# The last products of a two-layer trunk cut 384 and 128 tokens, with the final norm's weights multiplied on ScalarE

## The chip, the cores and the metric

The kernel runs on one core of a Trainium2 chip. The metric is the device time of one execution in microseconds (us), as the median of several runs. The profile shows one execution; its engines are PE (TensorE, matmuls), PEld (TensorE's weight loads, which overlap matmuls), DVE (VectorE), ACT (ScalarE), POOL (GpSimd) and SP (SyncE, here the queue that issues nearly all transfers).

## The reference

An input of 512 tokens x 1024 features passes through two layers: a token mixer (attention in the first, a gated recurrence in the second) and a squared-ReLU MLP after each. All of it is in float32. Only the end matters here, the second half of the last MLP and the final norm:

```python
def rmsnorm(x, g):
    y = xf * lax.rsqrt(jnp.mean(xf * xf, axis=-1, keepdims=True) + RMS_EPS)
    return (y * g.astype(jnp.float32)).astype(x.dtype)

    z = jax.nn.relu(jnp.einsum('bsd,df->bsf', h, w1))
    return jnp.einsum('bsf,fd->bsd', z * z, w2)      # D_FF = 4096
...
        h = h + sq_relu_mlp(rmsnorm(h, norm_mlp[layer]), mlp_w1[layer], mlp_w2[layer])
    return rmsnorm(h, norm_final)
```

## The kernel before

Features lie on the 128 partitions and tokens along the free dimension: the residual is eight tiles `hT[0..7]` of 128 features x 512 tokens. Every float32 operand of a product is split into a high part and a low rest, so one product of two blocks is three matmuls (`mm3`, lines 180 to 182), each with a weight load of 128 x 128 of its own.

An MLP runs over eight groups `g` of 512 hidden units. For each group `up(g)` makes the hidden units and `down(g - 1, m)` adds the group before it to the residual, with one projection for each feature tile `m` (line 624). In the last MLP the eighth group's down projection is written out apart (lines 665 to 689), because the final norm and the output follow it. The code is written in program order, and a scheduler orders the instructions of each engine in it from what they depend on.

There the 512 tokens are cut in two halves of 256 (`norms`, line 667). For each half and each tile `m` the projection makes 4 x 3 matmuls into one of four accumulator buffers (tag `mm`), VectorE adds the result to `hT` (line 685), and `Norm.square` squares it on ScalarE and adds it to a running sum on VectorE (lines 208 to 216). The last tile's square of the second half is made on VectorE and goes into the sums by matmuls of its own (`apart`, line 212; `last`, line 213).

`finish` then makes the norm of a half. `sums` adds over the features with matmuls against ones (line 232), ScalarE takes the root (line 236) and VectorE the reciprocal (line 237). `rstd` spreads the result over the partitions as a row with a matmul (line 243); for the first half ScalarE copies the row out of PSUM (line 247), for the second VectorE reads it there. For each tile VectorE multiplies residual, weight and row in one instruction (line 677), and after two tiles SP issues a store of 256 KB (line 678). The first half's `finish` comes after the second tile of the second half, and the second half's after everything. The running sums of both halves share one buffer (tag `nacc`).

Of the kernel before, what the change touches and what calls it, by code (L numbers as in the profile page):

```python
# [10 lines left out]
F32 = mybir.dt.float32  # L11
F32R = mybir.dt.float32r
AF = mybir.ActivationFunctionType
ALU = mybir.AluOpType

P = 128
T = 512
D = 1024
KT = D // P
NH = 16  # L20
HD = 64
U = 256
# [9 lines left out]
C_MIX0, C_MLP0, C_MIX1, C_MLP1, C_FIN = 0, 8, 16, 24, 32  # L32
# [8 lines left out]
def trunk(ctx: ExitStack, tc: tile.TileContext, xT, cols, win, wqkv, wo, rwin, rga, rgx, rwo, w1, w2, out):  # L41
    nc = tc.nc
    V, S, G, PE = nc.vector, nc.scalar, nc.gpsimd, nc.tensor
# [8 lines left out]
    def mmp(name):  # L52
        return ps.tile([P, T], F32, name=name, tag="mm")
# [5 lines left out]
    cst = per.tile([P, P], F32, name="cst")  # L59
    hT = [per.tile([P, T], F32, name=f"hT{k}") for k in range(KT)]  # L60
# [123 lines left out]
    def project(accs, cols_, WH, WL, xs, mid=None):  # L184

        for k, (XH, XL) in enumerate(xs):
            if mid and k == len(xs) // 2:
                mid()
            for acc, c in zip(accs, cols_):
                mm3(acc, WH(k, c), WL(k, c), XH, XL, k == 0, k == len(xs) - 1)  # L190
# [62 lines left out]
    with ExitStack() as actx:  # L253
# [169 lines left out]
        for k0, nk in FIRST:  # L423
            WH, WL = want(1)
            for k in range(k0, k0 + nk):
# [4 lines left out]
                for i in range(4):  # L430
                    c = slice(i * P, (i + 1) * P)
# [94 lines left out]
    def mlp(ly, norm, nxt, halves):  # L526
        with ExitStack() as mctx:
            pool = lambda name, bufs: mctx.enter_context(tc.tile_pool(name=f"{name}{ly}", bufs=bufs))
            sr, wx, tp, cp, zp = pool("sr", 1), pool("wx", 3), pool("t", 1), pool("c", 1), pool("z", 2)
# [123 lines left out]
            for g in range(1, 8):  # L653
                m = 0
# [9 lines left out]

            ws = [want(1) for u in range(4)]
            tc.keep_in_program_order(S.activation(spare, epsb, AF.Sqrt))
            norms = [Norm(f"nf{h}", C_FIN, h * U, U) for h in range(2)]

            def finish(nf):
                nf.sums()  # L670
                rf = nf.rstd()
                for m in range(0, KT, 2):
                    o = sr.tile([P, 1024], F32, name=f"{nf.name}o{m}", tag=("b11", "b21", "b22", "b12")[m // 2])
                    o = o[:, :T].rearrange("p (i c) -> p i c", i=2)
                    for i in range(2):
                        g = cst[:, C_FIN + m + i : C_FIN + m + i + 1]
                        V.scalar_tensor_tensor(o[:, i], hT[m + i][:, nf.c], g, rf, ALU.mult, ALU.mult)
                    nc.sync.dma_start(out[m * P : (m + 2) * P, nf.c].rearrange("(k p) c -> p k c", p=P), o)

            for h, nf in enumerate(norms):  # L680
                for m in range(KT):
                    acc = mmp(f"d{ly}7{m}{h}")[:, :U]
                    WH, WL = ws[m // 2]
                    project([acc], [PAIR[m % 2]], WH, WL, [(z[7, k][0][:, nf.c], z[7, k][1][:, nf.c]) for k in range(4)])
                    V.tensor_add(hT[m][:, nf.c], acc, hT[m][:, nf.c])
                    nf.square(m, h == 1 and m == KT - 1)
                    if h and m == 1:
                        finish(norms[0])
            finish(norms[1])

    n1 = Norm("n1", C_MIX1)
    mlp(0, nm1, n1.feed, False)


    nm2 = Norm("nm2", C_MLP1, late=True)
    with ExitStack() as rctx:
# [83 lines left out]
        for u in range(4):  # L780
            WH, WL = want(2)
            for i in range(2):
                c = 2 * u + i
                if i == 1 and u < 3:
                    gate_weights(u + 1)
                acc = mmp(f"xb{c}")
# [13 lines left out]
        for u in range(4):  # L800
            WH, WL = want(2)
            for i in range(2):
                c = 2 * u + i
# [15 lines left out]
        for u in range(4):  # L819
            WH, WL = want(2)  # L820
            accs = [mmp(f"ro{2 * u + i}") for i in range(2)]
            for i in range(2):
                m = 2 * u + i
# [5 lines left out]
                nm2.feed(m)  # L829

    mlp(1, nm2, None, True)


# [35 lines left out]
```

## Time and profile before

| | |
|---|---|
| median of 3 runs | 1092.68 us (1092.35 to 1092.8) |
| the profiled execution | 1092.29 us, of which the span from the first to the last instruction is 1090.5 us |
| busy share of the span | PE 99%, PEld 87%, DVE 79%, ACT 49%, POOL 1% |
| granted TensorE clock, mean of the span | 0.997 of full speed |
| transfers | 109 MB in 113784 packets |

A matmul's row shows its start and a modelled length that overlaps the next; the distance from one start to the next tells what it costs in a stream. The rows below give times from the start of the span. In a timeline row stand the start, the length, the engine, the line, the operation, the tiles written and read, and the shapes, partitions x elements; for PE the shape after the arrow is what is moved. Rows that say x4 merge four neighbours.

### The profile page before, as it was taken

What the parts mean: (1) busy time and instruction counts of PE and PEld (TensorE: products, weight loads), DVE (VectorE), ACT (ScalarE), POOL (GpSimd) and SP (SyncE); (2) the same over time, 40 slices, a digit from 0 to 9 for tenths busy, and PEclk for the clock granted to TensorE, in tenths of its full rate; (3) what the DMA queues carried; (4) which work ended last, traced back from release to release, by engine and by line L of the source; (5) the groups of instructions that cost most, each with busy time, mean ns of one, the idle gap of its engine ahead of it and who ended that gap; (6) DMA issues with size and microseconds to landing.
All of it is one profiled execution on the core that took longest, in us unless ns stands there. A gap on an engine that the chain in (4) does not pass through costs nothing.

```text
span 1090.5 us, 15782 instructions
## 1 busy us (share of the span) xinstructions
PE 1074.5 (99%) x6280; PEld 951.5 (87%) x6280; DVE 857.6 (79%) x1284; ACT 534.1 (49%) x778; POOL 10.5 (1%) x28
## 2 busy tenths in 40 slices
PE   9999999999999999999999999899999999999996
PEld 7889989878999999899988888788998999999896
DVE  7997888879777786786776889969777777786765
ACT  7766666566443443342344688446343443443321
POOL 1000000000000000000000000000000000000000
PEclk9999999999999999999999999999999999999998
DMA  8532432341432323322242222531532432322102
GB/s 270 138 100 76 116 104 71 95 156 48 146 116 78 109 91 109 98 84 91 78 135 59 78 71 65 168 122 58 156 97 78 124 102 84 109 91 90 61 1 78
DMA packets 113784, 109.08 MB, mean 100 GB/s; under 512 B 4016, under 2 KB 110640, under 8 KB 113712
## 3 DMA queue, kind: packets, MB, share of 16 engines
q1 hardware_dynamic: 113568, 108.02, 32.5%
q8 instruction: 49, 0.80, 0.3%
q14 instruction: 23, 0.19, 0.1%
q10 hardware_dynamic: 144, 0.07, 0.0%
HBM read 101.78 MB, written 2.10 MB: 95 GB/s over the span
## 4 chain that ended last, share of the span: by engine, by line
PE 87%; DVE 8%; ACT 2%; DMA 1%; issue 1%; DVEq 0%; SPq 0%; ACTq 0%
PE d L180 11%; PE d L181 11%; PE d L182 10%; PE p L182 9%; PE p L181 9%; PE p L180 9%; DVE wl L119 1%; PE u L180 1%; PE xb L180 1%; PE xb L182 1%; PE u L182 1%; PE u L181 1%; PE xb L181 1%; PE x L380 1%; PE wo L181 1%
## 5 line engine op out<-in xcount | busy, mean ns | idle before, releaser
L118 ACT CAST wh<-wr 128x1024 fp32r<-128x1024 f32 (+1 forms) x129 | 134.4, 1044 | 217.2 <-PE d L181 95.1
L181 PE MATMUL d<-zL,wh 128*128 128x512 f32 (+1 forms) x544 | 205.7, 379 | 0.0
L180 PE MATMUL d<-zH,wh 128*128 128x512 f32 (+1 forms) x544 | 205.5, 379 | 0.0
L182 PE MATMUL d<-zH,wl 128*128 128x512 f32 (+1 forms) x544 | 204.5, 377 | 0.0
L118 ACT CAST wh<-b 128x1024 fp32r<-128x1024 f32 x98 | 101.8, 1051 | 164.6 <-PE p L181 91.1
L119 DVE TENSOR_TENSOR wl<-wr,wh 128x1024 fp32r<-128x1024 f32 (+1 forms) x129 | 156.6, 1214 | 26.5 <-ACT wh L118 22.5
L119 DVE TENSOR_TENSOR wl<-b,wh 128x1024 fp32r<-128x1024 f32 x98 | 118.7, 1222 | 35.3 <-ACT wh L118 35.2
L182 PE MATMUL p<-tH,wl 128*128 128x256 f32 x448 | 126.8, 283 | 0.0
L181 PE MATMUL p<-tL,wh 128*128 128x256 f32 x448 | 126.8, 283 | 0.0
L180 PE MATMUL p<-tH,wh 128*128 128x256 f32 x448 | 126.6, 282 | 0.0
L182 PEld LDWEIGHTS d<-zH,wl 128*128 128x128 f32 x544 | 102.4, 188 | 19.4
L180 PEld LDWEIGHTS d<-zH,wh 128*128 128x128 f32 x544 | 102.5, 189 | 17.0 <-ACT zH L570 0.4
L181 PEld LDWEIGHTS d<-zL,wh 128*128 128x128 f32 x544 | 102.7, 189 | 15.7
L624 DVE TENSOR_TENSOR hT<-d,hT 128x512 f32<-128x512 f32 x120 | 82.6, 688 | 42.5 <-PE d L182 42.0
L182 PE MATMUL p<-hnH,wl 128*128 128x256 f32 x336 | 95.1, 283 | 0.0
L181 PE MATMUL p<-hnL,wh 128*128 128x256 f32 x336 | 95.1, 283 | 0.0
L180 PE MATMUL p<-hnH,wh 128*128 128x256 f32 x336 | 94.9, 282 | 0.0
L181 PEld LDWEIGHTS p<-tL,wh 128*128 128x128 f32 x448 | 85.8, 192 | 1.6
L180 PEld LDWEIGHTS p<-tH,wh 128*128 128x128 f32 x448 | 85.8, 192 | 1.6
L182 PEld LDWEIGHTS p<-tH,wl 128*128 128x128 f32 x448 | 85.8, 192 | 0.0
L181 PEld LDWEIGHTS p<-hnL,wh 128*128 128x128 f32 x336 | 64.3, 191 | 1.6
L180 PEld LDWEIGHTS p<-hnH,wh 128*128 128x128 f32 x336 | 64.3, 191 | 1.6
(334 smaller groups left out, 2146.5 us busy)
## 6 DMA issues: line engine op xcount, KB each, us to landing
wr<-in_w SPq DMA_DIRECT2D x72, 512.0 KB, 3.5
b<-in_w SPq DMA_DIRECT2D x56, 512.0 KB, 4.5
wr<-in_wqkv SPq DMA_DIRECT2D x20, 512.0 KB, 4.0
wr<-in_rwin SPq DMA_DIRECT2D x16, 512.0 KB, 3.5
wr<-in_wo SPq DMA_DIRECT2D x8, 512.0 KB, 3.5
wr<-in_rwo SPq DMA_DIRECT2D x8, 512.0 KB, 3.5
hT<-in_xT SPq DMA_DIRECT2D x8, 256.0 KB, 4.8
bias<-in_win SPq DMA_DIRECT2D x4, 512.0 KB, 4.4
```

What stands on the lines that cost most here:

```text
L118: S.copy(H[:, :n], raw[:, :n])
L119: V.tensor_sub(L[:, :n], raw[:, :n], f(H[:, :n]))
L180: PE.matmul(acc, WH, XH, start=start, stop=False)
L181: PE.matmul(acc, WH, XL, start=False, stop=False)
L182: PE.matmul(acc, WL, XH, start=False, stop=stop)
L380: PE.transpose(b[:, c : c + P], pt[:, seg[t] + kt * P : seg[t] + (kt + 1) * P], ident)
L624: V.tensor_add(hT[m], acc, hT[m])
```

## The change

The last down projection's cut becomes 384 and 128 tokens. The multiplication by the final norm's weights moves ahead of the norm: as soon as a tile of the residual is final, ScalarE writes tile x weight into the output buffer (`scale`). `finish` then multiplies the buffer by the row only, in place, over several feature tiles at once: two tiles x 384 tokens in the first part, four tiles x 128 tokens in the second. The first part's four buffers are the same as before, now 768 columns each; the second part uses the two buffers `cA` and `cB` of the hidden units. The first part's four stores are issued on SP's queue. Of the second part's two stores of 256 KB the first is issued on SP's queue and the second on ScalarE's.

```diff
-            norms = [Norm(f"nf{h}", C_FIN, h * U, U) for h in range(2)]
-
-            def finish(nf):
+            cuts = ((0, T - P), (T - P, P))
+            norms = [Norm(f"nf{h}", C_FIN, c0, n) for h, (c0, n) in enumerate(cuts)]
+
+            def finish(nf, step):
                 nf.sums()
                 rf = nf.rstd()
-                for m in range(0, KT, 2):
-                    o = sr.tile([P, 1024], F32, name=f"{nf.name}o{m}", tag=("b11", "b21", "b22", "b12")[m // 2])
-                    o = o[:, :T].rearrange("p (i c) -> p i c", i=2)
-                    for i in range(2):
-                        g = cst[:, C_FIN + m + i : C_FIN + m + i + 1]
-                        V.scalar_tensor_tensor(o[:, i], hT[m + i][:, nf.c], g, rf, ALU.mult, ALU.mult)
-                    nc.sync.dma_start(out[m * P : (m + 2) * P, nf.c].rearrange("(k p) c -> p k c", p=P), o)
+                for n, m in enumerate(range(0, KT, step)):
+                    o = scaled[nf][m // step]
+                    V.tensor_mul(o, o, rf[:, None, :].to_broadcast([P, step, nf.n]))
+                    eng = nc.scalar if nf.last is not None and n else nc.sync
+                    eng.dma_start(out[m * P : (m + step) * P, nf.c].rearrange("(k p) c -> p k c", p=P), o)
+
+            def scale(nf, m):
+
+                o = scaled[nf]
+                step = KT // len(o)
+                S.activation(o[m // step][:, m % step], hT[m][:, nf.c], AF.Copy, scale=cst[:, C_FIN + m : C_FIN + m + 1])
+
+            scaled = {norms[0]: [], norms[1]: []}
+            for m, tag in enumerate(("b11", "b21", "b22", "b12")):
+                o = sr.tile([P, 1024], F32, name=f"nf0o{m}", tag=tag)[:, : 2 * (T - P)]
+                scaled[norms[0]].append(o.rearrange("p (i c) -> p i c", i=2))
+            for m, tag in enumerate(("cA", "cB")):
+                o = cp.tile([P, 2, T], F32, name=f"nf1o{m}", tag=tag)[:, 0]
+                scaled[norms[1]].append(o.rearrange("p (i c) -> p i c", i=4))
 
             for h, nf in enumerate(norms):
                 for m in range(KT):
-                    acc = mmp(f"d{ly}7{m}{h}")[:, :U]
+                    acc = mmp(f"d{ly}7{m}{h}")[:, : nf.n]
                     WH, WL = ws[m // 2]
                     project([acc], [PAIR[m % 2]], WH, WL, [(z[7, k][0][:, nf.c], z[7, k][1][:, nf.c]) for k in range(4)])
                     V.tensor_add(hT[m][:, nf.c], acc, hT[m][:, nf.c])
                     nf.square(m, h == 1 and m == KT - 1)
+                    scale(nf, m)
                     if h and m == 1:
-                        finish(norms[0])
-            finish(norms[1])
+                        finish(norms[0], 2)
+            finish(norms[1], 4)
```

## Rows read from the trace of the kernel before

**Rows 1.** The page: busy time of each engine, share of the span, instructions.
```profile
PE 1074.5 (99%) x6280; PEld 951.5 (87%) x6280; DVE 857.6 (79%) x1284; ACT 534.1 (49%) x778; POOL 10.5 (1%) x28
```

**Rows 2.** Busy time by stretch: length, then busy us of each engine, granted clock, DMA.
```profile
core 0: us, PE busy (x) PEld busy (x) DVE busy (x) ACT busy (x) POOL busy (x), PEclk, DMA share, GB/s
1055.77:1080.08 24.31, 24.30 (x201) 23.98 (x199) 15.96 (x38) 6.90 (x19) 0.00 (x0) 1.00 0.13 44
...
1083.50:1090.48 6.98, 0.00 (x0) 0.00 (x0) 3.22 (x8) 0.00 (x0) 0.00 (x0) 0.60 0.46 150
```

**Rows 3.** The chain of waits from 1070 us: start, us, what.
```profile
1072.89 3.26 DVE nf0o L677 x8
...
1080.90 0.43 DVE nf1sq L212
...
1081.38 0.84 PE nf1ss L232 x6
...
1082.76 0.72 PE nf1row L243 x4
...
1083.51 0.48 DVE nf1o L677
```

**Rows 4.** Timeline of PE before the last products, at their ends, in the sums.
```profile
1054.18 0.39 PE L182 MATMUL d<-zH,wl 128*128 128x512 f32 x1
...
1055.77 0.28 PE L180 MATMUL d<-zH,wh 128*128 128x256 f32 x1
...
1079.96 0.28 PE L182 MATMUL d<-zH,wl 128*128 128x256 f32 x1
...
1081.62 0.36 PE L232 MATMUL nf1ss<-ones,nf1acc 128*128 128x2 f32 x2
1081.84 0.36 PE L232 MATMUL nf1ss<-ones,nf1sq 128*128 128x2 f32 x2
```

**Rows 5.** Timeline of PE in the scores of one attention head.
```profile
109.52 0.22 PE L349 MATMUL s<-kl,q 128*128 128x128 f32 x1
109.58 0.28 PE L350 MATMUL s<-kh,q 128*128 128x128 f32 x1
...
109.98 0.34 PE L349 MATMUL s<-kl,q 128*128 128x384 f32 x1
110.16 0.34 PE L350 MATMUL s<-kh,q 128*128 128x384 f32 x1
110.34 0.39 PE L349 MATMUL s<-kl,q 128*128 128x512 f32 x1
```

**Rows 6.** Timeline of weight loads in the transposes of one attention head.
```profile
112.85 1.12 PEld L380 LDWEIGHTS x<-ident,p 128*128 128x128 f32 x10
113.94 0.19 PEld L180 LDWEIGHTS v<-wh,hnH 128*128 128x128 f32 x1
```

**Rows 7.** Groups by line and shape: busy us, mean ns of one, idle before.
```profile
L624 DVE TENSOR_TENSOR hT<-d,hT 128x512 f32<-128x512 f32 x120 | 82.6, 688 | 42.5 <-PE d L182 42.0
L685 DVE TENSOR_TENSOR hT<-d,hT 128x256 f32<-128x256 f32 x16 | 6.6, 423 | 2.4 <-PE d L182 2.1
...
L315 ACT ACTIVATE v<-v,rt 128x128 fp32r<-128x128 f32 x32 | 11.2, 367 | 11.6 <-DVE v L316 10.2 <-PE v L182 1.3
L215 ACT ACTIVATE nf1sq<-hT 128x256 f32<-128x256 f32 x6 | 2.4, 418 | 5.2 <-DVE hT L685 4.8 <-DVE nf1acc L216 0.4
```

**Rows 8.** Timeline: a tile's last matmul and its add, first half; last add.
```profile
1067.31 0.28 PE L182 MATMUL d<-zH,wl 128*128 128x256 f32 x1
...
1067.63 0.42 DVE L685 TENSOR_TENSOR hT<-d,hT 128x256 f32<-128x256 f32 x1
...
1080.44 0.42 DVE L685 TENSOR_TENSOR hT<-d,hT 128x256 f32<-128x256 f32 x1
```

**Rows 9.** GB/s in 40 slices: 1083.50 to 1090.50 (stores), 133.50 to 136.50 (512 B loads).
```profile
GB/s 0 0 0 0 0 0 0 0 0 0 187 369 334 328 287 334 339 345 287 369 334 339 304 345 357 345 328 363 100 0 0 0 0 0 0 0 0 0 0 0
...
GB/s 0 0 0 0 0 34 48 82 96 96 96 171 239 280 328 287 328 314 341 369 335 341 348 355 341 355 348 341 321 307 226 164 96 7 0 0 0 0 0 0
```

**Rows 10.** Timeline of SP from 1083 us: the issues of the last stores.
```profile
1084.41 2.72 SPq L678 DMA_DIRECT2D out<-nf1o  x4
```

## The prediction

> **What bounds the kernel now.** I read the busy line of the page first: the matmul row is busy for 99% of the span [rows 1], so up to the last matmul TensorE's stream of instructions sets the time. Busy matmuls are not a measure of work done, so what counts below is the distance between starts. Next the table by stretch, cut at the last projection [rows 2]. The two halves of the last products take 24.31 us, at a granted clock of 1.00 (2.4 GHz). After them 10.4 us pass with little matmul: 3.42 us in which the norm's sums and row are made, and 6.98 us with no matmul, in which VectorE forms the last outputs and they are stored. The chain of waits [rows 3] names what follows what in this tail: the squares of the last tile, the sums, the row, then VectorE's products. It also shows eight such products for the first half (3.26 us) inside the second half's stream: VectorE is nearly as full there as TensorE. So the change is judged in two places: how long the products last, and how long the tail behind them is.
>
> **The products.** Each half issues 8 tiles x 4 parts x 3 = 96 matmuls, every one with a weight load of its own. From the first of 256 tokens (1055.77) to the last (1079.96) [rows 4] are 191 steps in 24.19 us; 1.27 us of it is where sums, row and a short wait cut in, the rest is 0.120 a step. Seven steps of 512 tokens lead up to 1055.77 in 1.59 us, 0.227 each [rows 4]. Cutting 512 tokens as 384 and 128 leaves the columns the same, so the question is what a step of each width costs.
>
> *384 tokens.* The attention scores have such matmuls: two steps from 109.98 to 110.34, 0.18 each [rows 5]. Halfway between 0.120 and 0.227 is 0.1735. The scores' steps of 512 are a little over 0.227 too, so I take 0.175. 96 x (0.175 - 0.120) = +5.28 us; with 0.1735 and 0.18 it is +5.14 and +5.76.
>
> *128 tokens.* Here a step cannot be half of 0.120 if the weight load is what spaces it. The transposes of attention load 128 x 128 for each 128 columns moved: ten loads from 112.85 to 113.94 [rows 6], 0.109 each. Against that stand two score matmuls of 128 tokens that start 0.06 apart [rows 5]; but the first of them had found its weights loaded during a long matmul, which happens once, not 96 times in a row. I take 0.110: 96 x (0.110 - 0.120) = -0.96 us; with 0.109 and 0.112 it is -1.06 and -0.77. So the narrow product is hardly shorter than the half it replaces, while the wide one grows in full.
>
> The Trainium skill, page "TensorE: Matmul & The Clock Gate", says two things on this. Under "LDWEIGHTS (loading the stationary operand)" a load lasts its columns divided by 1.2 GHz, 107 ns for 128, which the loads' 0.109 bears out. Under "Back-to-back issue gap" a sustained stream with 128 columns runs at about 81 ns, which no row here shows; by that figure the narrow product would last 7.8 us instead of 10.6, and the sum below would be -0.4 us instead of +2.4.
>
> *Sums and row of the first part.* Three groups of 128 tokens instead of two: two more instructions in the sums and two more in the row. From 1081.62 to 1081.84 two sums' instructions take 0.22 [rows 4], and in the row a step is much the same (four in 0.72 [rows 3]), so +0.22 and +0.22, both in TensorE's stream. Products together: 5.28 - 0.96 + 0.44 = **+4.76 us**, from 4.52 to 5.43.
>
> **The tail.** It is cut for 128 tokens.
> - The last add to the residual and the last squares stand in series. VectorE takes 0.423 for 256 tokens and 0.688 for 512 [rows 7], so 0.13 less for each 128: -0.26 us.
> - The sums: from 1081.38 to the last pair there are three pairs in series, 0.84 us [rows 3]. With one group only the squares' pair is left behind the squares, -0.46. The row has two instructions for four, -0.22. Together -0.68. The root and the reciprocal between them stay.
> - The outputs. Before, the eight VectorE products start at 1083.51 and the store's traffic ends near 1088.5: in the view of transfers from 1083.50, 40 slices of 0.175 us, it fills slices 11 to 29 [rows 9]. That is 5.0 us. Now the norm's weights are already in, and one multiplication covers four tiles x 128 = 512 columns, 0.69 as in [rows 7]. The first issue came 0.03 after its data and the first traffic 0.87 after the issue (1084.41 [rows 10] to about 1085.28), so the first 256 KB starts at 0.69 + 0.90 = 1.59 and the second, one multiplication later, at about 2.2. The old store ran at about 335 GB/s with runs of 1 KB; now a run is 512 B. Loads with such runs reach 340 GB/s in their middle but rise and fall slowly [rows 9]. At full rate 512 KB is 1.57 us and the end is at 3.2; with such edges up to 3.9. I take 3.5: -1.5 us, from -1.8 to -1.1.
> - The second queue: an SP issue is over long before the second data is ready (four issues in 2.72 us, spaced by VectorE [rows 10]), so moving the second store to ScalarE's queue costs and brings nothing; ScalarE's queue is empty behind the root by then. If the issue there is slower, the bound of 3.9 holds it.
>
> Tail: -0.26 - 0.68 - 1.5 = **-2.44 us**.
>
> **What lies beside.** ScalarE gets 16 multiplications by the weights. It is busy for 6.90 of 24.31 us in the products [rows 2], and one for 128 columns takes 0.367 [rows 7]; for 384 I estimate 0.6 from that and the 0.418 of 256. Beside a square in each tile's 2.1 us of the wide product this is hidden. VectorE's first outputs become four multiplications of 768 columns, about 0.9 each by the slope above, 3.5 us for 3.26. They start later: sums, row and copy for three groups add about 0.5. After the second tile of the narrow product follow sums and that chain, so the block ends some 9.3 us behind the wide product, and TensorE ends at about 10.6 + 1.14 + 0.44 = 12.1. VectorE then has 2.8 us for ten adds of 128 tokens at under 0.29, which just fits. Before it was as tight: the last add started 0.48 after its matmul (1079.96 to 1080.44), where 0.32 was usual (1067.31 to 1067.63) [rows 8], so 0.16 late. I put the change of this lateness at +0.1, from -0.16 (it vanishes) to +0.5. The stores of the first part (1.5 MB, some 4.7 us) begin with that block and end before the last outputs start; if they did not, the last store would wait for them. Four accumulator buffers cover VectorE's block for TensorE, as they did.
>
> **Sum.** 4.76 - 2.44 + 0.1 = +2.4 us. The profiled execution took 1092.29 us (span 1090.5), so 1094.7; the runs' median is 1092.68, 0.39 above it, so **1095.1 us**. The bounds give 4.52 - 0.26 - 0.68 - 1.8 - 0.16 = +1.6 and 5.43 - 0.26 - 0.68 - 1.1 + 0.5 = +3.9, so 1094.3 to 1096.6. About 0.2% (2.2 us) is what a measurement of this kernel can tell from no change, and the sum stands just beyond it.
>
> **Rivals.**
> - *The narrow product is cheap.* If a step of 128 tokens costs 0.06, as the two scores [rows 5], TensorE saves another 4.8 us. For it speaks only that pair, against it every chain of loads [rows 6]. Not all of it would be had: VectorE's block would start only 1.2 us earlier (24 steps x 0.05), and with the ten adds behind it VectorE would set the end. So the end comes 1.2 earlier, or up to 2.4 if the adds get ahead of the block: 1092.7 to 1093.9, not slower. It decides from a step of about 0.108 down, since the sum is 0.2 us past the line. By the page's 81 ns (the section on the issue gap above) 2.8 us would be saved, which the same bound cuts to 2.4, so 1092.7.
> - *VectorE and ScalarE hold the last product.* Behind the block each tile needs a square (under 0.418) and a weight multiplication (0.367) on ScalarE. If the multiplications stand ahead of the squares, five tiles are 3.3 to 3.9 us against the 2.8 that are left: the last add comes 0.7 to 1.6 late, 1095.8 to 1096.7. The tight fit speaks for it; against it that squares stand ahead in the code.
> - *The wide product is hidden behind VectorE.* The chain of waits passes through VectorE in the second half [rows 3], so one could hold TensorE's steps for free. But the lateness is only 0.16 us; it cannot hide 5.
>
> **Chances.** The sum as worked out 0.58 (0.36 of it beyond 2.2 us, 0.22 within), the cheap narrow product 0.15 (0.12 within 0.2%, 0.03 faster), the held last product 0.17 (slower), the rest 0.10, of which 0.06 within and 0.04 faster. So slower 0.53, same 0.40, faster 0.07. The range takes in the bounds and most of the cheap product: 1093.2 to 1096.8; by itself the likeliest case is 1094.3 to 1096.6.
>
> **What would show it.** Right: steps near 0.175 and 0.11 in the two products, the last matmul 4.5 to 5.4 us later than now, and 2 to 3 us less from there to the end, two multiplications of about 0.69 in it. Wrong: narrow steps well under 0.1; a granted clock under 1.00 in the narrow product; ScalarE's root or VectorE's last add waiting on the weights' multiplications; the last 512 KB lasting longer than 2 us.

## The result, and the profile after

The changed kernel's median is 1095.84 us over 11 runs, before 1092.52 over 11 runs beside them. The ratio over all runs is 1.0048, 95% interval [1.0035, 1.0061], or +5.2 us: slower, as forecast, by twice the +2.4 of the sum. The median lies where it was expected, but it is the median of two groups. Seven executions take 1094.65 to 1096.8 us (median 1095.49; mean granted clock 0.997 to 0.998), four take 1101.96 to 1102.44 (mean clock 0.989). Nothing lies between them, so no single time describes this kernel.

The profiled execution (1101.96 us) is of the second group. Its page answers to [rows 1] with the same fullness of TensorE, and the last of the 40 slices shows where the clock went:

```profile
span 1100.1 us, 15781 instructions
PE 1086.0 (99%) x6278; PEld 963.1 (88%) x6278; DVE 855.9 (78%) x1274; ACT 539.8 (49%) x794; POOL 10.4 (1%) x28
PEclk9999999999999999999999999999999999999995
```

The table by stretch, cut finer than [rows 2] (columns as there), finds the place. The wide product ends at 1072.4, and then:

```profile
1055.80:1072.00 16.20, 16.20 (x94) 16.07 (x94) 8.82 (x15) 7.16 (x16) 0.00 (x0) 1.00 0.00 0
1072.00:1076.00 4.00, 4.00 (x37) 4.00 (x36) 1.86 (x5) 1.79 (x5) 0.00 (x0) 1.00 0.02 4
1076.00:1080.00 4.00, 3.65 (x20) 3.54 (x20) 1.87 (x4) 1.24 (x5) 0.00 (x0) 0.61 0.00 0
1080.00:1084.00 4.00, 4.00 (x21) 4.00 (x20) 3.14 (x7) 1.09 (x4) 0.00 (x0) 0.50 0.90 319
1088.00:1092.00 4.00, 4.00 (x20) 4.00 (x20) 0.87 (x3) 0.95 (x4) 0.00 (x0) 0.50 0.00 0
```

The clock column falls from 1.00 (2.4 GHz) to 0.50 (1.2 GHz) within 1076 to 1080 and stays there to the end, though TensorE is busy nearly throughout (3.65 of 4 us, then all of it); 37 matmuls in 4 us become 20. Cut into half microseconds the column is 1.00 up to 1076.5 and 0.50 from 1077.0. The timeline of PE shows the steps on either side, and what stands at the fall:

```profile
1070.12 0.33 PE L182 MATMUL d<-zH,wl 128*128 128x384 f32 x1
1070.29 0.34 PE L180 MATMUL d<-zH,wh 128*128 128x384 f32 x1
...
1072.54 0.27 PE L182 MATMUL d<-zH,wl 128*128 128x128 f32 x1
1072.65 0.28 PE L180 MATMUL d<-zH,wh 128*128 128x128 f32 x1
...
1075.00 0.78 PE L232 MATMUL nf0ss<-ones,nf0acc 128*128 128x2 f32 x6
...
1076.63 1.42 PE L243 MATMUL nf0row<-ident,rt 128*128 128x128 f32 x6 [0.35 <-DVE rt L237]
1077.70 0.45 PE L181 MATMUL d<-zL,wh 128*128 128x128 f32 x1
...
1078.17 0.41 PE L180 MATMUL d<-zH,wh 128*128 128x128 f32 x1
1078.38 0.41 PE L181 MATMUL d<-zL,wh 128*128 128x128 f32 x1
...
1092.03 0.41 PE L182 MATMUL d<-zH,wl 128*128 128x128 f32 x1
```

Steps of 384 are 0.17 apart and narrow ones 0.11, as forecast. Then the first part's sums (two columns each), four narrow steps, a standstill of 0.35 us and the row interrupt the stream. I call these the break; the clock falls as the row begins, right behind the standstill. From 1077.70 to 1092.03 are 67 steps in 14.33 us, 0.214 each: 0.103 more than before the break, so 6.9 us. That is about the distance between the groups (6.7 us from median to median).

Behind the products the chain of waits answers to [rows 3], with two sums' instructions for six, two of the row for four, and one multiplication of 0.69 ahead of the store:

```profile
1092.48 0.30 DVE hT L698
1092.81 0.30 DVE nf1sq L212
1093.16 0.60 PE nf1ss L232 x2
1093.78 0.27 ACT rt L236
1094.30 0.81 PE nf1row L243 x2
1095.13 0.69 DVE nf1o L675
```

From the last add to the end of the span are 7.62 us (1092.48 to 1100.1), before 10.06 (1080.44 [rows 8] to 1090.5): -2.44, as the sum had it, on a clock at half. The store's traffic (GB/s in 40 slices, 1095.10 to 1100.10) answers to [rows 9] and ends near 1098.6, 3.5 us after 1095.13, as taken, at some 290 GB/s:

```profile
GB/s 0 0 0 0 0 0 0 0 0 0 0 0 0 53 279 295 279 233 311 336 287 275 291 287 283 295 295 279 119 0 0 0 0 0 0 0 0 0 0 0
```

### The profile page after: what moved, and what is told of

It reads as the page before. It is cut to its first block, busy times and chain, and to the rows that moved or that the text cites. A ratio compares the mean times of both kernels' runs of the same rounds, so it can differ in the third digit from the quotient of the medians.

```text
span 1100.1 us, 15781 instructions
## 1 busy us (share of the span) xinstructions
PE 1086.0 (99%) x6278; PEld 963.1 (88%) x6278; DVE 855.9 (78%) x1274; ACT 539.8 (49%) x794; POOL 10.4 (1%) x28
## 4 chain that ended last, share of the span: by engine, by line
PE 88%; DVE 7%; ACT 2%; DMA 1%; issue 1%; DVEq 0%; SPq 0%; ACTq 0%
PE d L180 11%; PE d L181 11%; PE d L182 11%; PE p L182 9%; PE p L181 9%; PE p L180 9%; PE u L180 1%; PE xb L180 1%; DVE wl L119 1%; PE xb L182 1%; PE u L182 1%; PE u L181 1%; PE xb L181 1%; PE x L380 1%; PE wo L180 1%; PE wo L181 1%
## 5 line engine op out<-in xcount | busy, mean ns | idle before, releaser
L181 PE MATMUL d<-zL,wh 128*128 128x512 f32 (+2 forms) x544 | 210.1, 387 | 0.0
L180 PE MATMUL d<-zH,wh 128*128 128x512 f32 (+2 forms) x544 | 210.0, 387 | 0.0
L182 PE MATMUL d<-zH,wl 128*128 128x512 f32 (+2 forms) x544 | 209.0, 385 | 0.0
L182 PEld LDWEIGHTS d<-zH,wl 128*128 128x128 f32 x544 | 105.5, 194 | 19.5
L180 PEld LDWEIGHTS d<-zH,wh 128*128 128x128 f32 x544 | 105.6, 194 | 16.9 <-ACT zH L570 0.4
L181 PEld LDWEIGHTS d<-zL,wh 128*128 128x128 f32 x544 | 105.8, 195 | 15.7
```

Of the source, the lines that this page charges most:

```text
L180: PE.matmul(acc, WH, XH, start=start, stop=False)
L181: PE.matmul(acc, WH, XL, start=False, stop=False)
L182: PE.matmul(acc, WL, XH, start=False, stop=stop)
```

## The experiments

**The question** is what drops the clock in the narrow product. My theory: narrow steps and the break together. Rivals: narrow steps alone do it, whatever stands between them; or the break does it, whatever the steps around it; or it is chance, of an occasion or a chip. A second question is why executions without the fall still exceed the sum a little.

**e1_again, e12_again: the changed kernel, unedited**, on two more occasions.

> The changed kernel once more, nothing edited. Theory A (the few columns moved per weight load in the narrow product let the clock fall, in some executions): two groups of times again, one near 1095.5 us with a mean clock of 0.997 to 0.998, one near 1102 us with 0.989. Where the clock stays at 1.00, the steps are 0.175 and 0.110 and the sum of the prediction holds (1095.1). Rival B (the standstill before the norm's row in the narrow product makes it fall) and rival C (a disturbance from outside, as the same kernel may meet at any time): B the same two groups, C times near 1095.5 in all or nearly all executions.

> The changed kernel, unedited, on the chip that runs the filled one. If the fall comes of the kernel, some of its executions (about four in ten so far) lie near 1102 here, and the others near 1095.5; if it came of the chips used before, none does, and the filled kernel's times prove nothing.

e1: 1095.07 to 1096.12 (4 runs), 1098.84 (1), 1101.96 and 1102.14; ratio 1.0047 [1.0029, 1.0065]. e12: 1095.04 to 1096.49 (7 runs), 1102.81 (1); ratio 1.0035 [1.0018, 1.0052]. With the first 11 runs, 7 of 26 lie near 1102 and one between. The fall belongs to the kernel, not to an occasion. The profiled execution of e1 has no fall in the narrow product, with the same break in it:

```profile
1076.00:1080.00 4.00, 3.65 (x33) 3.54 (x33) 2.06 (x4) 1.43 (x5) 0.00 (x0) 1.00 0.00 0
1080.00:1084.00 4.00, 4.00 (x38) 4.00 (x38) 3.15 (x8) 1.41 (x6) 0.00 (x0) 1.00 0.95 336
1084.00:1088.00 4.00, 2.62 (x18) 2.37 (x17) 1.93 (x8) 2.16 (x7) 0.00 (x0) 0.78 0.16 58
```

It is the execution to hold against the sum. Its products run from 1055.92 to 1085.13, 29.21 us for 24.19: +5.02. But its last add starts 0.97 us after that matmul. The timeline of DVE says why:

```profile
1084.03 0.29 DVE L216 TENSOR_TENSOR nf1acc<-nf1acc,nf1sq 128x128 f32<-128x128 f32 x1 [0.44 <-ACT nf1sq L215]
1084.24 0.28 DVE L698 TENSOR_TENSOR hT<-d,hT 128x128 f32<-128x128 f32 x1
1084.96 0.29 DVE L216 TENSOR_TENSOR nf1acc<-nf1acc,nf1sq 128x128 f32<-128x128 f32 x1 [0.44 <-ACT nf1sq L215]
...
1086.10 0.28 DVE L698 TENSOR_TENSOR hT<-d,hT 128x128 f32<-128x128 f32 x1
```

Each add to the residual (`hT`) is queued behind the running sum of the tile before it (`nf1acc`), which waits for ScalarE's square, which waits for that tile's add. So a tile costs 0.93 us (1084.03 to 1084.96), though VectorE is busy for only half of it, and the queue that VectorE's block left (the four multiplications of the first part's outputs, 3.56 us) is not worked off in time.

**e2_wide: twice the columns in the narrow product.** Each matmul moves 256 tokens, of which the first 128 results are thrown away.

```diff
-                    acc = mmp(f"d{ly}7{m}{h}")[:, : nf.n]
+                    full = mmp(f"d{ly}7{m}{h}")
+                    cols = nf.c if h == 0 else slice(T - U, T)
+                    moved = full[:, : cols.stop - cols.start]
+                    acc = moved[:, cols.stop - cols.start - nf.n :]
...
-                    project([acc], ...[(z[7, k][0][:, nf.c], z[7, k][1][:, nf.c]) for k in range(4)])
+                    project([moved], ...[(z[7, k][0][:, cols], z[7, k][1][:, cols]) for k in range(4)])
```

> The narrow product moves 256 columns for each weight load and throws the first 128 away; sums, row and standstill stay. A: the clock stays at 1.00 in every execution, the steps go from 0.110 to 0.120, so 96 x 0.010 = +1.0 us over the undisturbed changed kernel: 1096 to 1097 in all of them, none near 1102, although TensorE does twice the work. B and C: some executions still fall to the half clock, near 1102 or above.

1095.09 us median, 11 runs from 1094.4 to 1095.66, ratio 1.0019 [1.0011, 1.0028]. More work made the kernel faster and steadier: no execution lies near 1102. But the break did not stay whole, as had been expected. The timeline of PE:

```profile
1075.42 0.73 PE L232 MATMUL nf0ss<-ones,nf0acc 128*128 128x2 f32 x6
...
1076.81 0.28 PE L180 MATMUL d<-zH,wh 128*128 128x256 f32 x1
1077.00 0.91 PE L243 MATMUL nf0row<-ident,rt 128*128 128x128 f32 x6
```

Sums and row are there, but between them stand seven steps of 256 columns instead of four narrow ones, and the standstill is gone. So e2 shows that sums and row among steps of 256 columns leave the clock up; it takes away the narrow width and the standstill together and cannot tell them apart.

Other traces of the same kernels can. The norm ahead of the first layer has the same break, sums, standstill and row, in a stream of 512 columns a step. Here it is in the changed kernel's profiled execution, with the table by stretch:

```profile
23.93 0.95 PE L232 MATMUL n0ss<-ones,n0acc 128*128 128x2 f32 x8
...
26.64 0.39 PE L182 MATMUL qk<-hnH,wl 128*128 128x512 f32 x1
27.82 1.13 PE L243 MATMUL n0row<-ident,rt 128*128 128x128 f32 x8 [0.79 <-DVE sp L501]
```

```profile
24.00:34.00 10.00, 9.21 (x62) 8.17 (x61) 8.67 (x22) 7.42 (x10) 1.25 (x4) 1.00 0.72 205
```

The standstill is longer than the one in the narrow product, and the clock stays at 1.00. All fourteen profiled executions have this place, with a standstill of 0.24 to 0.93 us, and in none does the clock fall there. So such a break does not drop the clock whatever the steps around it: the narrow steps have their part. A standstill among steps of 256 columns was not tried.

That e2 also came in below the 1096 to 1097 us expected has another reason. In its trace the last matmul starts at 1085.43 (e1: 1085.13), but the scheduler put three adds ahead of the running sums, and the last add waits for TensorE alone:

```profile
1081.94 0.68 DVE L701 TENSOR_TENSOR hT<-d,hT 128x128 f32<-128x128 f32 x3
...
1085.75 0.29 DVE L701 TENSOR_TENSOR hT<-d,hT 128x128 f32<-128x128 f32 x1 [0.39 <-PE d L182]
...
1087.88 1.28 DVE L675 TENSOR_TENSOR nf1o<-nf1o,nf1row 128x512 f32<-128x512 f32 x2 [0.58 <-PE nf1row L243]
```

From the last add to the outputs are 2.13 us here against 2.62 in e1 (1086.10 to 1088.72). In e1 the clock had fallen by the time of the late sums and row (0.80 us for its two instructions), in e2 not yet (0.49). So e1 pays 0.65 us of lateness and then 0.5 of half clock. That the lateness brings the half clock is not shown: the clock falls 1.1 us after the start of the last product step in e1, 2.5 us in e2 and 4.9 us in the kernel before.

**e3_late: no break.** The first part's `finish` stands behind the narrow product (with a running sum of its own for the second part).

```diff
...
-                    if h and m == 1:
-                        finish(norms[0], 2)
+            finish(norms[0], 2)
             finish(norms[1], 4)
```

> The first part's sums, row and outputs come after the narrow product instead of inside it, so that its 96 steps follow each other without any break. A: the clock still falls within the narrow product in some executions, steps of 0.213 after it. B: it never falls there. With the clock up 10.6 us for the narrow product, and then the first part's outputs in the open: 1.6 us less in the products, some 5 more behind them, near 1099; with the clock down up to 7 more.

1097.21 to 1098.45 us in 5 runs, median 1097.73, ratio 1.0046 [1.0034, 1.0058]. In the profiled execution all 96 narrow steps run at 1.00. The kernel is some 2 us slower than e1's profiled execution, because the first part's outputs no longer lie under the products, but not the 3.5 us that had been expected. The edit takes more out of the narrow product than the break: VectorE's block and the first part's stores go too. Neither is what drops the clock: it falls in e7 without the block, and in the changed kernel's profile the stores' traffic starts only at 1080, after the fall.

**e5_twice: e3 with twice the narrow steps**, 192 in a row.

```diff
-                    project([acc], ...
+                    for _ in range(1 + h):
+                        project([acc], ...
```

> As the late run, with the first part's sums and outputs behind the products, but each tile of the narrow product is computed twice over (its eight tiles come out double, so the output is not the reference's): 192 narrow steps in one unbroken stretch of 21 us. A (narrow steps alone let the clock fall): the granted clock falls to half inside that stretch in some executions, which adds up to 15 us. B (it needs the break by sums and row as well): the clock is 1.00 through all 192 steps in every execution, one group of times, 10.6 us above the late run, near 1108.3.

1108.07 to 1110.9 us in 4 runs, ratio 1.0148 [1.0135, 1.0161]. (Each of the two passes starts its accumulator anew, so the tiles do not come out double; the time is not touched by that.) The table by stretch, late in the doubled product:

```profile
1088.00:1092.00 4.00, 4.00 (x38) 4.00 (x38) 0.88 (x3) 0.76 (x3) 0.00 (x0) 1.00 0.02 4
1092.00:1096.00 4.00, 4.00 (x38) 4.00 (x38) 0.88 (x3) 1.05 (x4) 0.00 (x0) 1.00 0.00 0
```

Some 20 us of unbroken narrow steps leave the clock at 1.00 here, and none of the nine executions of e3 and e5 lies 6 us above the others of its kernel. Narrow steps alone are therefore very unlikely to be enough (chances under "The count").

**e10_sums: e3 with the first part's sums back inside**, without standstill and row.

```diff
...
+                    if h and m == 1:
+                        norms[0].sums()
...
```

> As e3 (the first part's row and output after the narrow product), but with the first part's column sums, six matmuls of two columns, back inside the narrow product, so that neither the standstill nor the row breaks it. If the sums alone are enough for the clock to fall, some of the executions should be 6 to 7 us above the others; if it takes the standstill or the row as well, all should lie near e3's 1097.7 with the clock at 1.00 until the last product has ended.

1096.55 to 1099.79 us in 5 runs, median 1097.78, ratio 1.0045 [1.0032, 1.0059]. None is 6 us above the others, and the profiled one keeps 1.00 through the product. Its 2 us above e3 come from elsewhere (last section). Five runs miss a fall that comes in a third of executions with a chance of 0.12, or 0.51 at the one in eight of this chip (e12), so this hardly leans towards standstill and row.

**e9_fill, e11_fill: the break filled.** Six matmuls of 512 columns that nothing reads stand between sums and row.

```diff
                 nf.sums()
+                if nf.last is None:
+                    fill = atp("fill")
+                    for i in range(6):
+                        PE.matmul(fill, ws[1][0](0, PAIR[0]), z[7, 0][0], start=True, stop=True)
```

> The changed kernel with six more matmuls of 512 columns, whose result nothing reads, put on TensorE between the first part's column sums and its row, where TensorE stands still for 0.35 us. If the clock falls because the break in the narrow product (two-column sums, standstill, row) leaves TensorE with little to do among steps of 128 columns, it should now stay at 1.00 through the narrow product in every execution, and the times lie in one group at 1095 to 1096.5 (1.3 us more on TensorE, most of which waits for VectorE anyway). If the break counts by the order of work alone, about four executions in ten should still lie near 1102.

> The kernel of e9 (six unread matmuls of 512 columns behind the first part's sums) once more, beside the unedited changed kernel on the same chip: e9 had five executions, all at 1096.1 to 1096.7, and five can miss a fall that comes four times in ten (0.6 to the fifth is 0.08). If the filled break keeps the clock up, all of these stay below 1098 as well; if e9 was luck or its chip, some lie near 1102 to 1103.

e9: 1096.1 to 1096.71 (5 runs), ratio 1.0032 [1.0019, 1.0044]; e11: 1095.62 to 1097.09 (6 runs), ratio 1.0032 [1.002, 1.0045]. The timeline of PE of e9 shows the fill in the place of the standstill, and its table by stretch the clock:

```profile
1074.94 0.78 PE L232 MATMUL nf0ss<-ones,nf0acc 128*128 128x2 f32 x6
1075.58 1.64 PE L675 MATMUL fill<-zH,wh 128*128 128x512 f32 x6
1077.06 0.83 PE L243 MATMUL nf0row<-ident,rt 128*128 128x128 f32 x6
```

```profile
1076.00:1080.00 4.00, 4.00 (x33) 3.78 (x32) 2.03 (x4) 1.19 (x5) 0.00 (x0) 1.00 0.00 0
```

None of the 11 executions falls. On this chip the unedited kernel fell only once in eight (e12), so these runs alone do not decide (0.23 for 11 without a fall at that rate); they agree with the theory. Sums and row are in them, among narrow steps; the standstill is gone.

**e6_cut: the cut 384 and 128 alone** on the finish of before.

```diff
-            norms = [Norm(f"nf{h}", C_FIN, h * U, U) for h in range(2)]
+            cuts = ((0, T - P), (T - P, P))
+            norms = [Norm(f"nf{h}", C_FIN, c0, n) for h, (c0, n) in enumerate(cuts)]
...
```

> The cut into 384 and 128 tokens alone; weights, outputs and queue as in the kernel before. Sum: products +4.8 to +5.0, the tail without the shorter multiplications saves less (eight of 128 columns, about 2.1 us for 3.2, and four stores of 128 KB), VectorE's first block gets longer (8 x 0.53 = 4.2 us). With the clock up 1095.5 to 1096.5, so the other edits bring at most 1 us in the changed kernel; in some executions the clock falls, near 1102 to 1103. If the other edits were what hurts, this would be near the kernel before.

1096.38 and 1096.64, and 1102.89 to 1103.18 in four runs; ratio 1.0072 [1.0051, 1.0093]. The cut brings both the cost and the two groups.

**e7_nomul: the first part's four row multiplications left out.**

```diff
-                    V.tensor_mul(o, o, rf[:, None, :].to_broadcast([P, step, nf.n]))
+                    if nf is norms[1]:
+                        V.tensor_mul(o, o, rf[:, None, :].to_broadcast([P, step, nf.n]))
```

> The changed kernel without the first part's four multiplications by the row (its 384 tokens come out unnormalised); everything else stays, the stores too. Theory: VectorE's block of 3.5 us is what makes the last add 0.65 late while the clock is up, so the last add starts 0.32 instead of 0.97 after its last matmul, and undisturbed executions come to 1094.8 to 1095.0. Rival: the squares' and weights' cycle between VectorE and ScalarE of 0.93 us a tile is late by itself, then the lateness stays. Where the clock falls it stays near 1102, since TensorE then sets the end.

1094.32 to 1095.01 in 8 runs (median 1094.61), 1102.32 to 1102.67 in 4; ratio 1.0034 [1.0016, 1.0053]. Without the block the executions without the fall stand 1.6 us above the kernel before that ran beside them (1093.05), those of the changed kernel 2.8 to 3.0 above theirs: VectorE's queue costs about 1.3 us, near the two parts of lateness under e2 (0.65 and 0.5). The fallen ones gain nothing, and falls come as often, so VectorE's lateness is not what drops the clock.

**e4_halves, e8_pairs: all but the cut.** Weights on ScalarE, two queues, 256 and 256 tokens; e4 multiplies four tiles at once in the second half, e8 two in both and stores from SP and ScalarE in turn.

```diff
-            cuts = ((0, T - P), (T - P, P))
+            cuts = ((0, U), (U, U))
...
```

> The cut goes back to 256 and 256; weights on ScalarE, the row on two tiles (first half) and four tiles (second half) and the two queues stay. A and the prediction's sum: products as before (24.3 us), the clock at 1.00, one group of times. At the end a multiplication of 1024 columns lasts 1.22, so the first store starts 0.3 later than before and 1 MB still takes 3.3: 1092.5 to 1093, no change within 0.2%. Rival: the other edits have a cost of their own (ScalarE's queue, in-place multiplication), then 1094 or more.

> 256 and 256 tokens, weights on ScalarE, the row on two tiles at once in both halves, the second half's stores alternately on SP's and ScalarE's queue. First block on VectorE 2.6 us instead of 3.3, so the last add is not late (-0.16); the first store can be issued after 0.69 instead of 0.87 (-0.2). 1092.3 to 1092.6 against 1092.8, at the edge of what can be told; clock 1.00 through the products.

e4: 1092.56 us, ratio 0.9997 [0.9988, 1.0006]. e8: 1092.48 us, ratio 0.9994 [0.9986, 1.0003]. Each had 11 runs, within 1.4 us of each other, and none fell. Without the cut the other edits cannot be told from no change. No version beats the kernel before.

**The count.** Near 1102 lie 15 of 44 executions with narrow steps and the break (changed kernel 7 of 26, e6 4 of 6, e7 4 of 12). Take away the narrow width, and with it the standstill (e2), and it is 0 of 11; take away the break (e3, e5), 0 of 9; fill it, 0 of 11. If falls came as often there, the three would have chances of 0.01, 0.02 and 0.01. With the rates of the chips that they ran on the first two stay at 0.02, but the third is 0.23, so the filled break is the weakest of the three. With halves of 256 it is 0 of 22 (e4, e8), and none of the 79 executions of the kernel before lies 3 us above its median. In the first layer's break, among steps of 512, it is 0 of 14 traces, a chance of 0.003.

## Why the prediction was right and wrong

**What failed: the clock under the narrow product.** The term "96 x (0.110 - 0.120) = -0.96 us" took one step length for all 96, that is, the clock of [rows 2] for a stream that no longer was that of [rows 2]. In the profiled execution 67 of those steps last 0.214, +6.9 us; by their times 15 of 44 executions have this fall, and the ratio of 1.0048 contains about a third of the 6.9 us. "A granted clock under 1.00 in the narrow product" was named among the things that would show the sum wrong, but it had no chance, no price and no place in the range. The rows that could have priced it were at hand: a granted clock of 0.60 in the tail [rows 2] said that it falls where TensorE has little to do, and the change put a break between the steps with the fewest columns. That it takes both is what e3 and e5 on the one side and the first layer's break on the other point to. Why some executions pass the same break at 1.00 stays open. Which piece of the break counts stays open too: of the three, only the standstill stands in the narrow product of every kernel that fell and of none that did not, but narrow steps with a standstill and neither sums nor row were not tried.

**Products, +4.76: measured +5.02** (e1, no fall). The 384-token steps are a little cheaper than taken (0.173, +5.1 for +5.28) and the narrow ones as taken (0.111). The rest is the break: sums, standstill and row cost 0.7 more than before, for 0.44. The rival "the narrow product is cheap" is refuted. The 81 ns of the Trainium skill's page "TensorE: Matmul & The Clock Gate" ("Back-to-back issue gap") do not hold for these steps; that page's 107 ns for a load under "LDWEIGHTS (loading the stationary operand)" fit their 0.111 us. e2 shows from the other side that the columns are not what spaces them: with twice as many a step takes 0.120 us, and the products, with the standstill filled, last 29.65 us for 29.21 (1055.78 to 1085.43).

**Tail, -2.44: right as a sum, by other parts.** Adds, squares, sums and row were to give -0.94. From last add to first output it was 3.07 before (1080.44 [rows 8] to 1083.51 [rows 3]); it is 2.13 in e2, -0.94 exactly, where the clock is still up, but 2.65 in the changed kernel's profile and 2.62 in e1, where it is at half. The outputs were to give -1.5 by the end of the traffic, and gave that. The span ends 1.5 us behind the traffic now and ended 2.0 behind it before, another -0.5 that I had not looked for. The two errors cancel, which is luck.

**Lateness, +0.1: measured +0.49** (0.65 late for 0.16). The step "2.8 us for ten adds of 128 tokens at under 0.29, which just fits" counted VectorE's busy time and not what stands between its instructions. What went into it was right: the block takes 3.56 us for 3.5 and ends 9.3 us behind the wide product (e1: 1081.97), as taken. The second rival had the place right and the mechanism wrong: not weights ahead of squares, but adds behind running sums that wait for ScalarE.

**The sum without the fall.** 5.02 + 0.49 - 2.44 = +3.1 for +2.4; e1's profiled execution took 1095.56 us, +3.27 on 1092.29. The rival "the wide product is hidden" is refuted by the same +5.02. The second queue brought nothing that can be told, as said: the issues stand at 1095.89 on SP and 1096.50 on ScalarE, and e4 and e8, with both, are where before is. It was not taken away by itself.

## What to carry to other kernels

Before cutting a product narrow, compare its columns with its weight load: where every step has a load of its own, halving the columns may hardly shorten it, here to 0.111 us for 128 tokens from 0.120 for 256, and the wide remainder pays in full. A granted clock read from before holds for the stream of before: if an edit makes the steps narrow and leaves a break with a standstill among them, give "the clock falls" a price and a chance (here the rest of the product at twice the step, in a third of executions), and run it often enough to see groups. In a queue that must be worked off before the end, count the period of one tile through all engines, not the busy time of one.

## What had not been expected of the hardware

Making each narrow step move twice the columns (e2) made the kernel 0.3% faster in the mean over all runs. Another fall shows in the profiles of e10 and e5, in attention, where the kernel is that of before: TensorE stood still, in e5 for 2.13 us and in e10 for 1.64 us, waiting for a transfer, and then ran at half clock. e10 shows it (timeline of PE, then the table by stretch):

```profile
170.27 0.30 PE L350 MATMUL s<-kl,q 128*128 128x128 f32 x1 [1.64 <-DMA kl<-kl]
```

```profile
170.60:174.00 3.40, 3.40 (x16) 3.21 (x16) 2.50 (x12) 0.99 (x4) 0.00 (x0) 0.55 0.00 0
174.00:180.00 6.00, 6.00 (x50) 5.96 (x50) 2.60 (x7) 4.37 (x12) 0.00 (x0) 0.97 0.00 0
```

There the clock came back by itself while TensorE worked on, and the execution was 1.8 us above its kernel's median. In the narrow product it did not come back in over 14 us of full work.

The Trainium skill, page "TensorE: Matmul & The Clock Gate", section "What's actually happening", says that sustained activity gives the full clock back; attention agrees, the narrow product does not. The section also says that the gate watches activity on a schedule of its own, which no kernel starts, so that one kernel can meet it differently from run to run. Two groups of times are consistent with that; no run here shows the schedule.
